# Strassen's seven products for the first of the gMLP's four down projections

## The chip, the cores and the metric

One program runs on one core of a Trainium2 chip. The metric is the device time of one execution in microseconds (us); a lower number is better. TensorE is called PE in the profile, VectorE DVE, ScalarE ACT, GpSimd POOL and the engine that issues most loads SP.

## What is computed

The reference is a trunk of two layers for 512 tokens of width 1024. Each layer is a feed-forward block (FFN), a mixer, a second FFN and a gated input embedding, with a layer norm after each. The mixer of the second layer is the gMLP, the only part that the change touches:

```python
def gmlp_mixer(x, w_in, b_in, vn_g, vn_b, ws, bs, w_out):
    u, v = jnp.split(jax.nn.gelu(x @ w_in + b_in, approximate=False), 2, axis=-1)
    v = layer_norm(v, vn_g, vn_b).reshape(B, NB, GM_BLOCK, GM_GROUPS, GM_GDIM)
    ...
    s = jnp.einsum('gts,bnsgc->bntgc', ws_m, v) + bs.T[:, :, None]
    return (u * s.reshape(B, S, GM_WIDTH)) @ w_out
```

`u` and `v` are 512 x 2048, `w_out` is 2048 x 1024, and all data is float32.

## The kernel before, in words

**Arithmetic.** A float32 product is made of three fp32r matmuls: each operand is split into a high part (an ACT copy, `whi`, `hh`, `fhi`) and a rest (a DVE subtraction, `wlo`, `hl`, `flo`), and `mm3` multiplies high by high, high by low and low by high. One matmul takes a 128 x 128 stationary tile and a 128 x 512 moving tile.

**The gMLP.** First `v` is computed for all tokens into the tile `gvf` (128 partitions x 4 token blocks x 2048 features), with its gelu and its norm. Then 16 blocks b of 128 features follow. For each of them PE does the spatial product (`spatial`, psum `sps`, 16 small matmuls) and the projection of u (`gate_u`, psum `gups`, 24 matmuls, one block ahead). DVE puts the spatial product's scale and bias together (`gadd`, then four instructions into `gs`), splits the next but one block of `gvf` (`gvl` or `gv`), multiplies `gs` by `guf`, the gelu of u, and ACT and DVE split the product into `hh` and `hl` (`gated`). After blocks 3, 7, 11 and 15 `down` multiplies the four blocks just made by four row tiles of `w_out`: for each of four token blocks two psum banks (`dps`), four features blocks and `mm3`, which are 4 x 2 x 4 x 3 = 96 matmuls. DVE adds the banks to the residual `xt` (eight instructions of 128 x 512).

**Weights.** The class `Weights` holds the order of the weight tiles (`W.order`, made by `gm_weights`). A tile is 128 x 1024: a projection tile u_b, or a row tile of `w_out`. Two of them come in one load of 1 MB on SP's queue (`load`, L162) into one of three raw buffers (`RAW_BUFS = 3`). `fill` splits the next tiles in order into slots, four of the kind "main" and two of the kind "extra"; `stage_kinds` gives every tile its kind, by its place in groups of six. A slot comes free when PE has used its tile (`release`), so a split is written five or six tiles ahead of its use, and the place of `release` in the code is the place of the split in the queues of ACT and DVE. A load is written right behind the split that used up a raw buffer. With `low="dma"` the low part is not made by DVE: ACT writes minus the high part (L196), and a DMA on POOL's queue adds the raw tile to it (L197).

ACT, DVE, POOL and SP each take their instructions in the order of the code, and an instruction that waits holds those behind it.

**Strassen's products elsewhere.** The FFN and the mLSTM mixer already do their down projections as seven products of half-size blocks (`Group`, `Weights.forms`). A weight form is a sum or difference of quarter blocks of two raw loads, made in place on DVE (`t2` and `t1`, two instructions of 128 x 1024 each), then split. A feature form is made in place in the feature tile and split into `fhi` and `flo`. A `Group` has `form`, which makes the next feature form, `product`, which multiplies one feature form by one weight form (2 x 2 x 3 = 12 matmuls into two banks `gps`), and `add`, which adds the two banks to `xt` (two DVE instructions). There are two pairs of banks, used in turn, and products 2, 4, 5 and 6 are accumulated into a pair that holds an earlier one, so the add of product r - 2 is done before product r.

Of the kernel before, what the change touches and what calls it, by code (L numbers as in the profile page):

```python
# [16 lines left out]
P = 128  # L17
# [220 lines left out]
def hybrid_trunk(ctx: ExitStack, tc, x, p, ln_g, ln_b, ffn1_wgu, ffn1_wd, ffn2_wgu, ffn2_wd,  # L238
# [130 lines left out]

    def stage_kinds(first):  # L370

        n = len(W.order) - first
        for i in range(n):
            extra = i % 6 >= 4 if i < n // 6 * 6 else i >= n - 2
            W.order[first + i] = ("extra" if extra else "main",) + W.order[first + i][1:]

    def ml_weights():
        win, wout = ml_w_in[0], ml_w_out[0]
        first = len(W.order)
        for h in range(HEADS):  # L380
# [7 lines left out]
            if h:  # L388
# [3 lines left out]
                j0, j1 = W.add_load(kp(wout)[:, k:k + 2, :], 3), W.add_load(kp(wout)[:, k + 2:k + 4, :], 3, "gb")  # L392
                left, right = ((slice(None), slice(None), slice(c, c + 512)) for c in (0, 512))
                down_w = W.forms("", (j0, left), (j0, right), (j1, right), (j1, left))
# [9 lines left out]
    def gm_weights():  # L404
        win, wout = gm_w_in[0], gm_w_out[0]
        first = len(W.order)
        for c in range(4):
            add_wide(win, GW + c * 512)
        for b in range(16):
            if b in (0, 15):  # L410
                W.add((kp(win)[:, :, b * P:(b + 1) * P], [slice(None)]))
            elif b % 2:
                W.add((w_cols(win, b * P), cols2))
            if b and b % 4 == 0:
                add_rows(wout, b - 4, 4)
# [314 lines left out]
    class Group:  # L730
# [5 lines left out]
        def __init__(self, h, pool, first=False):  # L736
            self.h, self.pool, self.half = h, pool, h.shape[1] // 2
# [5 lines left out]
        def form(self):  # L743

            def a(i, j):
                m = self.half
                return self.h[:, m * j - m:m * j, (i - 1) * 256:i * 256]
# [16 lines left out]
        def product(self):  # L764
# [5 lines left out]
            for e, ps in enumerate(self.banks[r % 2]):  # L770
                for k in range(self.half):
                    mm3(ps, [a[:, k, e * P:(e + 1) * P] for a in f], [a[:, k] for a in w],
# [429 lines left out]
    def gmlp():  # L1202
        with stage_pool("extra", EXTRA) as extra, stage_pool("gm_parts") as near, stage_pool("ghpool", 4) as hpool, \
                stage_pool("gm") as mp:
# [109 lines left out]
            def gated(s, uf):  # L1314
                vec.tensor_mul(s, s, uf)
                h = new_h(hpool)
                split(h[0], h[1], s)
                return h
# [5 lines left out]
            for b in range(16):  # L1324
                if b in (0, 14):
# [10 lines left out]
                hs.append(gated(ss.popleft(), us.popleft()))  # L1336
                if ahead and b < 14:
                    W.release(low="dma")
                elif b == 15:
                    W.release()  # L1340
                if b % 4 == 3:
                    down(hs, b == 3, Norm(1, 1) if b == 15 else None)
                    hs = []
# [150 lines left out]
```

## Time and profile before

| | us |
|---|---|
| median of three runs (2232.39 to 2232.61) | 2232.42 |
| the profiled execution's own time | 2232.51 |
| its span, from the first to the last instruction | 2230.8 |
| PE busy in the span | 2220.3 |
| DVE busy | 1526.0 |
| ACT busy | 913.9 |
| POOL busy | 101.8 |

PE begins the projection of u_0 at 1621.2 us of the span, and the last matmuls of u_15 start at 1788.6. The rows of a timeline give the start, the busy time, the engine, the line, out<-in and the count. A DVE or ACT instruction's busy time overlaps the next one's start by some 0.1 us, so in a full queue the distance of two starts is the cost of one. What stands in brackets is how long the engine had been idle and what it waited for.

### The profile page before, as it was taken

To read this page: it belongs to the slowest core of one execution; us is meant where nothing else is said; L and a number is where in the kernel's file an instruction comes from. 1 tells how busy PE (TensorE), PEld (TensorE's weight loads), DVE (VectorE), ACT (ScalarE), POOL (GpSimd) and SP (SyncE) were. 2 spreads that over 40 slices of the span, in tenths; PEclk is the share of its full clock that TensorE was granted. 3 is DMA by queue.
4 is the path that set the end of the run, shared out by engine and by line. 5 is a ranking of instruction groups with operands and counts; after the bars stand their busy time and mean duration, and the time that the engine had idled before them with its cause. 6 is when DMAs were issued, how large, how long until landed. Compare 5 with 4: busy or idle time off the path is not lost.

```text
span 2230.8 us, 26548 instructions
## 1 busy us (share of the span) xinstructions
PE 2220.3 (100%) x10589; PEld 1864.0 (84%) x10589; DVE 1526.0 (68%) x2240; ACT 913.9 (41%) x1298; POOL 101.8 (5%) x135
## 2 busy tenths in 40 slices
PE   9999999999999999999999999999999999999998
PEld 8888888888888888888889888888888888888887
DVE  5666667777776786666687666666666578666677
ACT  4333336454646533333255333334343453333332
POOL 1000000111101100000000000000010100000000
PEclk9999999999999999999999999999999999999999
DMA  7422323466847443332233422223355443332221
GB/s 231 130 93 88 95 85 100 100 149 135 166 107 161 123 139 126 95 104 67 95 123 122 133 86 87 93 87 109 106 142 142 104 151 123 122 113 85 85 85 57
DMA packets 202723, 253.56 MB, mean 114 GB/s; under 512 B 5812, under 2 KB 156468, under 8 KB 202600
## 3 DMA queue, kind: packets, MB, share of 16 engines
q1 hardware_dynamic: 168080, 211.83, 29.5%
q0 software_dynamic: 27904, 25.35, 7.9%
q10 hardware_dynamic: 6616, 14.69, 2.0%
q8 instruction: 83, 1.36, 0.2%
q14 instruction: 40, 0.33, 0.0%
HBM read 224.58 MB, written 2.11 MB: 102 GB/s over the span
## 4 chain that ended last, share of the span: by engine, by line
PE 99%; ACT 1%; DVE 0%; issue 0%; DVEq 0%; POOL 0%; POOLq 0%
PE fps L269 13%; PE fps L270 13%; PE fps L268 13%; PE gps L270 7%; PE gps L269 7%; PE gps L268 7%; PE dps L269 3%; PE dps L268 3%; PE dps L270 3%; PE gups L268 1%; PE vps L268 1%; PE zps L268 1%; PE zps L270 1%; PE vps L270 1%; PE gvps L268 1%; PE gups L269 1%
## 5 line engine op out<-in xcount | busy, mean ns | idle before, releaser
L268 PE MATMUL fps<-xh,whi 128*128 128x512 f32 x1312 | 510.7, 389 | 0.0
L269 PE MATMUL fps<-xl,whi 128*128 128x512 f32 x1312 | 510.5, 389 | 0.0
L270 PE MATMUL fps<-xh,wlo 128*128 128x512 f32 x1312 | 510.4, 389 | 0.0
L199 DVE TENSOR_TENSOR wlo<-wraw,whi 128x1024 fp32r<-128x1024 f32 (+1 forms) x286 | 345.4, 1218 | 149.5 <-ACT whi L193 147.8
L193 ACT ACTIVATE whi<-wraw 128x1024 fp32r<-128x1024 f32 (+1 forms) x334 | 346.5, 1048 | 185.8 <-PE fps L269 81.6
L199 DVE TENSOR_TENSOR wlo<-wquarter,whi 128x1024 fp32r<-128x1024 f32 (+1 forms) x140 | 156.5, 1118 | 218.2 <-ACT whi L193 218.2
L268 PEld LDWEIGHTS fps<-xh,whi 128*128 128x128 f32 x1312 | 246.3, 188 | 51.2
L269 PEld LDWEIGHTS fps<-xl,whi 128*128 128x128 f32 x1312 | 246.3, 188 | 51.1
L270 PEld LDWEIGHTS fps<-xh,wlo 128*128 128x128 f32 x1312 | 246.2, 188 | 51.0
L193 ACT ACTIVATE whi<-wquarter 128x1024 fp32r<-128x1024 f32 (+1 forms) x140 | 136.3, 974 | 279.8 <-PE gps L270 209.0
L270 PE MATMUL gps<-whi,flo 128*128 128x512 f32 x588 | 229.3, 390 | 0.0
L268 PE MATMUL gps<-whi,fhi 128*128 128x512 f32 x588 | 229.3, 390 | 0.0
L269 PE MATMUL gps<-wlo,fhi 128*128 128x512 f32 x588 | 229.2, 390 | 0.0
L593 DVE TENSOR_TENSOR xt<-xt,gps 128x512 f32<-128x512 f32 x282 | 180.3, 680 | 0.5 <-PE gps L270 0.5
L817 ACT ACTIVATE sg<-fps 128x512 f32<-128x512 f32 x80 | 47.9, 598 | 228.4 <-PE fps L270 228.4
L273 ACT ACTIVATE fhi<-h 128x512 fp32r<-128x512 f32 (+1 forms) x140 | 80.5, 581 | 142.9 <-DVE h L755 54.4
L269 PEld LDWEIGHTS gps<-wlo,fhi 128*128 128x128 f32 x588 | 110.4, 188 | 23.5
L268 PEld LDWEIGHTS gps<-whi,fhi 128*128 128x128 f32 x588 | 110.4, 188 | 23.3
L270 PEld LDWEIGHTS gps<-whi,flo 128*128 128x128 f32 x588 | 110.4, 188 | 23.3
L274 DVE TENSOR_TENSOR flo<-h,fhi 128x512 fp32r<-128x512 f32 (+1 forms) x140 | 87.2, 634 | 42.9 <-ACT fhi L273 42.9
L563 POOL TENSOR_TENSOR rs<-rs,eps_pow 128x1 f32<-128x1 f32 x32 | 20.6, 643 | 1556.4 <-DVE rs L562 1556.4
L466 ACT ACTIVATE xf<-xps,cols 128x128 f32<-128x128 f32 x160 | 59.8, 453 | 52.5 <-PE xps L461 52.5
(289 smaller groups left out, 3736.4 us busy)
## 6 DMA issues: line engine op xcount, KB each, us to landing
wraw<-in_ffn_wgu_dram SPq DMA_DIRECT2D x79, 1024.0 KB, 6.0
wquarter<-in_ffn_wd_dram SPq DMA_DIRECT2D x64, 512.0 KB, 3.7
wraw<-in_ml_w_in_dram SPq DMA_DIRECT2D x24, 1024.0 KB, 5.5
wlo<-wraw POOLq DMA_DIRECT2D x48, 512.0 KB, 6.5
wraw<-in_gm_w_in_dram SPq DMA_DIRECT2D x15, 1024.0 KB, 5.7
wraw<-in_ffn_wgu_dram SPq DMA_DIRECT2D x17, 512.0 KB, 4.0
wraw<-in_ffn_wd_dram SPq DMA_DIRECT2D x8, 1024.0 KB, 4.9
wraw<-in_ml_w_out_dram SPq DMA_DIRECT2D x8, 1024.0 KB, 4.9
```

Of the source, the lines that this page charges most:

```text
L193: self.nc.scalar.activation(hi[:, s], src[:, s], AF.Copy)
L199: self.nc.vector.tensor_sub(lo[:, s], src[:, s], hi[:, s].bitcast(F32))
L268: mm(ps, st[0], mv[0], start=start, stop=False, skip_group_check=more)
L269: mm(ps, st[0], mv[1], start=False, stop=False, skip_group_check=more)
L270: mm(ps, st[1], mv[0], start=False, stop=stop, skip_group_check=more)
L273: sca.activation(hi, src, AF.Copy)
L274: vec.tensor_sub(lo, src, hi.bitcast(F32))
L466: sca.activation(xf[:, k], ps[:, k], AF.Identity, scale=col("ln_g", norm.at + 4 * g + k), bias=col("ln_b", norm.at + 4 * g + k))
L563: pool.tensor_tensor(rs[:, 1:2], rs[:, 0:1], eps_pow, op=OP.pow)
L593: vec.tensor_add(dst, dst, ps)
L817: sca.activation(sg, ps, AF.Silu)
```

## The change

The first `down` of the gMLP, that of blocks 0 to 3, is replaced by a `Group` of seven products that are spread over blocks 4 to 7 (`GM_STEPS`: 2, 2, 2 and 1). The gated features of blocks 0 to 3 are written back to their place in `gvf` in float32 and not split there. The seven feature forms are made from `gvf`; since `gvf` has the tokens as rows and the features as columns, `Group` gets the flag `by_tokens`, which changes the indices alone. In `gm_weights` the four row tiles of the first group go out and seven weight forms of two loads of `w_out` come in, behind u_5 (two), u_6 (two), u_7 (two) and u_8 (one). They are called f0 to f6 here, their products p0 to p6, and the two loads j0 and j1. In blocks 6 and 7 `gated` comes after the products ("late"), and the features of every third and fourth block are split into the tiles of the forms' pool, which takes the place of half of the pool `ghpool`. The other three `down` stay. `stage_kinds` gives the last four tiles of the stage their kinds in another way.

```diff
     def stage_kinds(first):
         n = len(W.order) - first
         for i in range(n):
-            extra = i % 6 >= 4 if i < n // 6 * 6 else i >= n - 2
+            extra = i % 6 >= 4 if i < n - 4 else i >= n - 2
...
+    def two_row_forms(w, kind="raw"):
+        j0, j1 = W.add_load(w[:, :2], 3), W.add_load(w[:, 2:], 3, kind)
+        left, right = ((slice(None), slice(None), slice(c, c + 512)) for c in (0, 512))
+        return W.forms("", (j0, left), (j0, right), (j1, right), (j1, left))
...
-            if b and b % 4 == 0:
+        tiles = W.order[at:]
+        del W.order[at:]
+        for b, tile_b in enumerate(tiles):
+            W.order.append(tile_b)
+            k = (b - 1) // 4 - 1
+            if b > 4 and k < GM_GROUPS:
+                if b % 4 == 1:
+                    down_w = deque(two_row_forms(kp(wout)[:, 4 * k:4 * k + 4, :]))
+                for _ in range(GM_STEPS[(b - 1) % 4]):
+                    W.order.append(down_w.popleft())
+            if b % 4 == 0 and b > 4 * GM_GROUPS:
                 add_rows(wout, b - 4, 4)
...
-            def gated(s, uf):
+            def gated(b, s, uf):
+                if b < 4 * GM_GROUPS:
+                    dst = vf[:, :, b * P:(b + 1) * P]
+                    vec.tensor_mul(dst, s.rearrange("p (t c) -> p t c", t=TB), uf.rearrange("p (t c) -> p t c", t=TB))
+                    return
                 vec.tensor_mul(s, s, uf)
-                h = new_h(hpool)
+                if b % 4 < 2:
+                    h = new_h(hpool)
+                else:
+                    h = [fpool.tile([P, 2, 256], F32R, name=n, tag=n).rearrange("p t c -> p (t c)") for n in ("fhi", "flo")]
                 split(h[0], h[1], s)
...
+            def step():
+                group.add()
+                group.product()
+                W.release(low="dma")
+                group.form()
...
             for b in range(16):
+                if group is not None:
+                    group.add()
...
-                hs.append(gated(ss.popleft(), us.popleft()))
+                late = group is not None and b >= 4 * GM_GROUPS and b % 4 >= 2
+                if not late:
+                    gated(b, ss.popleft(), us.popleft())
...
+                if group is not None:
+                    for _ in range(GM_STEPS[b % 4]):
+                        step()
+                if late:
+                    gated(b, ss.popleft(), us.popleft())
                 if b % 4 == 3:
-                    down(hs, b == 3, Norm(1, 1) if b == 15 else None)
-                    hs = []
+                    if group is not None:
+                        group.add()
+                        group = None
+                    if b < 4 * GM_GROUPS:
+                        group = Group(vf[:, :, (b - 3) * P:(b + 1) * P], fpool, b == 3, True)
+                        group.form()
+                        group.form()
+                    else:
+                        down(hs, False, Norm(1, 1) if b == 15 else None)
+                        hs = []
```

On PE the change takes out the 96 matmuls `dps` behind u_4 and puts 84 matmuls `gps`, twelve for each product, behind u_5, u_6, u_7 and u_8. Three other queues change their order at the first blocks.

**SP, the loads of the gMLP's weights.** `gm_w_in` are projection tiles, `gm_w_out` the rows of the down projection. Before:

```order
L162 DMA wraw_12748<-in_gm_w_in_dram 128x8x256
L162 DMA wraw_12807<-in_gm_w_out_dram 128x2x1024
L162 DMA wraw_12898<-in_gm_w_out_dram 128x2x1024
L162 DMA wraw_13039<-in_gm_w_in_dram 128x8x256
L162 DMA wraw_13050<-in_gm_w_in_dram 128x8x256
```

Now:

```order
L162 DMA wraw_12751<-in_gm_w_in_dram 128x8x256
L162 DMA wraw_12810<-in_gm_w_in_dram 128x8x256
L162 DMA wraw_12901<-in_gm_w_out_dram 128x2x1024
L162 DMA wraw_13042<-in_gm_w_out_dram 128x2x1024
L162 DMA wraw_13090<-in_gm_w_in_dram 128x8x256
```

The load of u_5 and u_6 (`wraw_12810`) has come ahead of the two loads of `gm_w_out`. The second of these, j1 (`wraw_13042`), now stands where the load of u_5 and u_6 stood (`wraw_13039`): it goes into the buffer of u_3 and u_4 (`wraw_12751`), once u_4 is split.

**ACT, from the gelu of u_0 on.** `whi` is the high part of a weight tile, `guf` the gelu of u, `hh` the high part of a gated block. Before:

```order
L1280 ACTIVATE guf_12991<-gups_12966,cols_108 128x512
L273 ACTIVATE gvh_13010<-gvf_12282 128x512
L273 ACTIVATE gv_13031<-gvf_12282 128x512
L193 ACTIVATE whi_13035<-wraw_12748 128x1024
L193 ACTIVATE whi_13041<-wraw_12807 128x1024
L193 ACTIVATE whi_13045<-wraw_12807 128x1024
L196 ACTIVATE wlo_13046<-wraw_12807 128x1024
L193 ACTIVATE whi_13052<-wraw_12898 128x1024
L196 ACTIVATE wlo_13053<-wraw_12898 128x1024
L273 ACTIVATE hh_13058<-gs_13005 128x512
L1280 ACTIVATE guf_13087<-gups_13062,cols_108 128x512
```

Now:

```order
L1305 ACTIVATE guf_12994<-gups_12969,cols_108 128x512
L273 ACTIVATE gvh_13013<-gvf_12285 128x512
L273 ACTIVATE gv_13034<-gvf_12285 128x512
L193 ACTIVATE whi_13038<-wraw_12751 128x1024
L193 ACTIVATE whi_13044<-wraw_12810 128x1024
L193 ACTIVATE whi_13048<-wraw_12901 128x1024
L193 ACTIVATE whi_13052<-wraw_13042 128x1024
L1305 ACTIVATE guf_13082<-gups_13057,cols_108 128x512
L193 ACTIVATE whi_13085<-wraw_12810 128x1024
L196 ACTIVATE wlo_13086<-wraw_12810 128x1024
L273 ACTIVATE gvh_13109<-gvf_12285 128x512
L1305 ACTIVATE guf_13138<-gups_13113,cols_108 128x512
```

The four splits are now those of u_4, u_5, f0 and f1. f1 reads j1, `wraw_13042`, and behind it stands the gelu of u_2 (`guf_13082`).

**DVE, from the low part of u_4 on.** Before, up to the gated product of block 2:

```order
L199 TENSOR_TENSOR wlo<-wraw,whi 128x1024 x2
L1315 TENSOR_TENSOR gs<-gs,guf 128x512
L274 TENSOR_TENSOR hl<-gs,hh 128x512
L1315 TENSOR_TENSOR gs<-gs,guf 128x512
L274 TENSOR_TENSOR hl<-gs,hh 128x512
L1303 SCALAR_TENSOR_TENSOR gadd<-rsum,cols 128x128
L1307 SCALAR_TENSOR_TENSOR gs<-sps,cols,gadd 128x256
L1309 SCALAR_TENSOR_TENSOR gs<-sps,cols,gs 128x256
L1307 SCALAR_TENSOR_TENSOR gs<-sps,cols,gadd 128x256
L1309 SCALAR_TENSOR_TENSOR gs<-sps,cols,gs 128x256
L274 TENSOR_TENSOR gvl<-gvf,gvh 128x512
L1315 TENSOR_TENSOR gs<-gs,guf 128x512
```

Now, up to the weight form f2 (`t2` is L105 and L106):

```order
L199 TENSOR_TENSOR wlo<-wraw,whi 128x1024 x4
L1343 TENSOR_TENSOR gvf<-gs,guf 128x4x128 x2
L1328 SCALAR_TENSOR_TENSOR gadd<-rsum,cols 128x128
L1332 SCALAR_TENSOR_TENSOR gs<-sps,cols,gadd 128x256
L1334 SCALAR_TENSOR_TENSOR gs<-sps,cols,gs 128x256
L1332 SCALAR_TENSOR_TENSOR gs<-sps,cols,gadd 128x256
L1334 SCALAR_TENSOR_TENSOR gs<-sps,cols,gs 128x256
L274 TENSOR_TENSOR gvl<-gvf,gvh 128x512
L1343 TENSOR_TENSOR gvf<-gs,guf 128x4x128
L105 TENSOR_TENSOR wraw<-wraw 128x2x512
L106 TENSOR_TENSOR wraw<-wraw 128x2x512
L199 TENSOR_TENSOR wlo<-wraw,whi 128x1024
```

DVE makes four low parts in a row where it made two, and the forms f2 and, a block later, f3 (`t1`, L110 and L111) stand between the blocks' own work. The low parts of the first two feature forms come behind f3.

22 lines of the change are left out of this document (13 added, 9 removed).

## The prediction

> **What bounds the kernel now.** I read the page first (the engines' shares and the chain that ended last), then the busy time by stretches of the gMLP.
>
> ```profile
> PE 2220.3 (100%) x10589; PEld 1864.0 (84%) x10589; DVE 1526.0 (68%) x2240; ACT 913.9 (41%) x1298; POOL 101.8 (5%) x135
> PE 99%; ACT 1%; DVE 0%; issue 0%; DVEq 0%; POOL 0%; POOLq 0%
> 1632.00:1653.00 21.00, 21.00 (x110) 17.98 (x109) 17.86 (x34) 16.06 (x22) 4.15 (x4) 1.00 0.63 159
> 1652.40:1674.20 21.80, 21.80 (x98) 18.06 (x97) 7.84 (x11) 6.29 (x7) 1.60 (x2) 1.00 0.77 168
> 1674.20:1699.80 25.60, 25.60 (x130) 21.76 (x129) 18.87 (x35) 12.56 (x17) 3.28 (x3) 1.00 0.59 160
> ```
>
> PE bounds it: no gap, and the chain is 99% PE. The stretches are blocks 0 to 3, the `down` that goes, and blocks 4 to 7; their columns are length, busy PE, PEld, DVE, ACT and POOL, granted clock, DMA share, GB/s. PE is full in all three. DVE is busy 85% of the first (17.86 of 21.00) and 74% of the third, but 36% of the `down`: that stretch, in which DVE catches up, is what the change takes away. So I ask when DVE and ACT deliver what p0 to p6 need.
>
> **The matmuls saved.**
>
> ```profile
> 1652.14 0.39 PE L270 MATMUL gups<-xh,wlo 128*128 128x512 f32 x1
> 1674.13 0.28 PE L1300 MATMUL sps<-wsp,gvh 128*128 128x256 f32 x1
> 1675.00 0.45 PE L268 MATMUL gups<-xh,whi 128*128 128x512 f32 x1
> ```
>
> Between the last matmul of u_4 and the next spatial product lie 96 matmuls `dps`: 97 steps in 21.99 us, 0.227 each. 12 fewer give 12 x 0.227 = **-2.7 us**. A product is 2.7, a projection of 24 matmuls 5.4, a spatial product 0.9 (1675.00 - 1674.13). With nothing waiting, u_4 ends at 1652.4, the spatial product at 1653.3, u_5 at 1658.7, and there p0 could begin.
>
> **The load that ACT waits for.** The rows of SP, ACT and DVE around u_4's split, and landing times of 1 MB loads issued alone and beside one of POOL's adding DMAs:
>
> ```profile
> 1634.76 2.94 ACT L193 ACTIVATE whi<-wraw 128x1024 fp32r<-128x1024 f32 x3
> 1638.22 2.35 DVE L199 TENSOR_TENSOR wlo<-wraw,whi 128x1024 fp32r<-128x1024 f32 x2
> 1639.46 6.46 SPq L162 DMA_DIRECT2D wraw<-in_gm_w_in_dram  x2
> wraw<-in_gm_w_out_dram SPq DMA_DIRECT2D x1, 1024.0 KB, 4.9
> wraw<-in_gm_w_out_dram SPq DMA_DIRECT2D x1, 1024.0 KB, 7.9
> 1670.30 1.06 ACT L193 ACTIVATE whi<-wraw 128x1024 fp32r<-128x1024 f32 x1 [14.63 <-PE dps L270]
> 1646.85 0.45 PE L268 MATMUL gups<-xh,whi 128*128 128x512 f32 x1
> ```
>
> A split's high part is 2.94 / 3 = 0.98 on ACT in a row, 1.06 alone. Before, the load issued at 1639.46, behind u_4's low part, was that of u_5 and u_6 and nobody was in a hurry for it. Now j1 is issued there, and f1's split is the fourth in a row on ACT, which reaches it at 1637.7. With 4.9 (no DMA of POOL's is under way then) j1 lands at 1644.4 and f1's high part ends at 1645.4. Behind it on ACT stand the gelu of u_2 and the split of block 4's v; the gelu ends at about 1646.1, and u_4, which takes u_2's bank at 1646.85 (the last row), isn't held. On DVE f1's low part stands ahead of everything for blocks 0 to 3.
>
> **What DVE and ACT then do before p0.**
>
> ```profile
> 1640.49 0.68 DVE L1315 TENSOR_TENSOR gs<-gs,guf 128x512 f32<-128x512 f32 x1
> 1644.47 0.35 DVE L1303 SCALAR_TENSOR_TENSOR gadd<-rsum,cols 128x128 f32<-128x128 f32 x1
> 1646.75 0.68 DVE L274 TENSOR_TENSOR gvl<-gvf,gvh 128x512 fp32r<-128x512 f32 x1
> 1647.35 0.69 DVE L1315 TENSOR_TENSOR gs<-gs,guf 128x512 f32<-128x512 f32 x1
> 1648.73 0.69 DVE L274 TENSOR_TENSOR hl<-gs,hh 128x512 fp32r<-128x512 f32 x1 [0.70 <-ACT hh L273]
> 1648.61 1.05 ACT L193 ACTIVATE whi<-wraw 128x1024 fp32r<-128x1024 f32 x1
> 1649.56 1.04 ACT L196 ACTIVATE wlo<-wraw 128x1024 fp32r<-128x1024 f32 x1
> 1650.51 0.62 ACT L273 ACTIVATE gv<-gvf 128x512 fp32r<-128x512 f32 x1
> L105 DVE TENSOR_TENSOR wraw<-wraw x3: 1218/1219/1220, 464.9 to 660.5; 128x1024 f32<-128x1024 f32 x3
> L755 DVE TENSOR_TENSOR h<-h 128x512 f32<-128x512 f32 x12 | 8.3, 692 | 0.4
> ```
>
> From starts: a low part of a weight tile is (1640.49 - 1638.22) / 2 = 1.15; a block's scaling and bias (`gadd` and four) 1646.75 - 1644.47 = 2.28; a 128 x 512 instruction 0.6 in a queue, 0.69 alone. `t2` or `t1` is two of 1.2, the second behind the first, 2.4. The row of L105 is of the mLSTM's forms, of the same shape; the sums for feature forms (L755) are in place as here.
>
> DVE from 1645.45: f1's low part 1.15; blocks 0 and 1 gated 1.2; block 2's scaling, v split and gating 3.5; `t2` 2.4; f2's split, high part first (1.05 on ACT, DVE waiting), 2.2; block 3's scaling, v split and gating 3.5; `t1` 2.4; f3's split 2.2; the first feature form's low part 0.7. Sum 19.2, so it is there at 1664.6. p0's third matmul needs it, and would have run at 1659.2: PE waits **5.4**. Of that 3.8 is j1: without it f1's low part would follow the three others at 1641.6 (1638.2 + 3 x 1.15).
>
> **Products 1 to 5.** p0 and p1 end at 1669.6, the next spatial product and u_6 at 1676.0. DVE meanwhile: block 4's scaling and v, 2.9, to 1668.0; then its gating, at whose start ACT's line begins: `hh` 0.7 later, u_7's high and minus part, f4's high part, 4.2 in all by the rows above (1650.51 + 1.04 - 1647.35), to 1672.2. f4's low part 1.15; two sums for feature form 2, 1.3, its high part on ACT 0.65, its low part 0.6; then p0's add. p2 adds into p0's banks, so it waits for the first of the add's two instructions, which ends 0.7 later, at 1676.7: wait **0.7**, and p2 ends at 1679.4. DVE goes on with the second (0.6), f5's low part (1.15), form 3's (0.6) and the first of p1's add (0.7), to 1679.7: p3 waits **0.3** and ends at 1682.4; the next spatial product and u_7 take PE to 1688.7. DVE: the second of p1's add 0.6, block 5's scaling and v 2.9, to 1683.2; its gating up to f6's high part 4.2; f6's low part 1.15, one sum 0.7, form 4 1.25, the first of p2's add 0.7: 1691.2. p4 waits **2.5** and ends at 1693.9. Then 0.6, a sum 0.7, form 5 1.3 and the first of p3's add 0.7: 1694.5, p5 waits **0.6**. Together 9.5. These waits are one line of DVE and ACT that runs from 1645 to 1694 in which each piece waits for the one before; p5 starts where it ends.
>
> **p6 and the second `down`.**
>
> ```profile
> wlo<-wraw POOLq DMA_DIRECT2D x48, 512.0 KB, 6.5
> wraw<-in_gm_w_in_dram SPq DMA_DIRECT2D x1, 1024.0 KB, 9.9
> wlo<-wraw POOLq DMA_DIRECT2D x1, 512.0 KB, 10.2
> ```
>
> The load of the last two row tiles of group 2 needs the buffer of u_7 and u_8, free when POOL's DMA has made u_8's low part: minus part done 3.2 behind the start of block 5's gating (1650.51 - 1647.35), at 1686.4, plus 6.5, 1692.9. It lands after 4.9 to 9.9, and I take 7.9, since another adding DMA is under way: 1700.8. ACT holds form 6's high part behind these splits, and with 3.95 for high part, minus part, form and the first of p4's add, p6 can start at 1704.7; PE, with p5 to 1697.2, a spatial product and u_8, is there at 1703.6: **1.1** (0 to 3.1). The low part of the last row tile then comes by DMA at 1711.8 to 1715.5 (1705.3 plus 6.5 to 10.2), and the `down` asks for it at 1711.5: I take **1.0** (0 to 4), near the lower end, which most of those DMAs show.
>
> A page of the Trainium skill speaks against this term: "DMA: Bandwidth & Descriptors", section "Anatomy of one DMA — SWDGE (gpsimd) path", gives such a DMA 2.0 us plus its bytes over 436 GB/s, by which 512 KB would take 3.2 us. By the page's figure both terms of this part would be nothing and the sum 2.1 lower. The row, 48 such DMAs of this kernel, has twice the page's time, so the terms above go by the row.
>
> **The stage's end.** `stage_kinds` leaves the last row tile as "extra", and its slot comes free only with u_15, so its split now stands behind the gating of block 15, where before it was done three blocks ahead.
>
> ```profile
> 1789.02 0.69 ACT L1280 ACTIVATE guf<-gups,cols 128x512 f32<-128x512 f32 x1 [4.20 <-PE gups L270]
> 1792.12 1.04 ACT L193 ACTIVATE whi<-wraw 128x1024 fp32r<-128x1024 f32 x1
> 1793.19 1.23 DVE L199 TENSOR_TENSOR wlo<-wraw,whi 128x1024 fp32r<-128x1024 f32 x1 [0.26 <-ACT whi L193]
> ```
>
> In the place of this split (of a later tile) its low part would be done at 1794.4. u_15 ends at 1788.95, the `down` needs the tile 19 matmuls later, at 1793.25: **1.2** (0.5 to 1.5).
>
> **Sum.** -2.7 + 9.5 + 1.1 + 1.0 + 1.2 = +10.1 on the profiled execution's 2232.51, which is 0.09 over the median: **2242.5**. What else the change adds (six more adds, three more weight splits, four sums) lies in DVE's line already or in the `down` of groups 2 to 4, where DVE is two thirds idle.
>
> **Rivals.**
> - *All of it is hidden*, not slower: 2232.5 - 2.7 = 2229.8, within 0.2%, which is about what a measurement can tell from no change here. For it: the FFN does such products with PE full. Against it: there each product has a projection to itself, here two share one, in a stretch with DVE at 74 to 85%. It decides at p0: DVE's line would have to be 5.4 shorter there and 9.5 by p5. 0.11.
> - *j1 holds nobody* (it is there in time) and the rest stays: 3.8 less, 2238.7. Against it: the place of j1 behind u_4's split on SP. 0.10.
> - *PE slows after its wait.* No row before has PE idle that long, and the granted clock is 1.00 in every stretch. If p0 and p1 ran at half pace, 24 matmuls would cost 5.4 more; the waits at p2, p3 and p4 (3.5) would take most of that up, so +1.9 at most, 2244.4. "TensorE: Matmul & The Clock Gate", in "Part 1: The HAM clock gate" of the Trainium skill, says that an idle window of some 3.4 us halves PE's clock until a busy one has passed. 0.09.
> - The forecast itself: 0.70.
>
> Slower by over 0.2% (over 2236.9) are the forecast, the second rival and the third, 0.89, with 0.02 taken off for waits much shorter than I worked out: 0.87. Within 0.2% are the first and half of those: 0.12. The saving is 0.12%, so faster by over 0.2% needs a gain that no row shows: 0.01. The range takes the lower ends of the last three terms (2239.7 with 0, 0 and 0.5) and the second rival (2238.7, and 2235.9 with those ends too): 2236.5. Above, it takes p6 and the `down` at 3.1 and 3.0: 2246.5.
>
> **What would show it.** Right: PE idle 5 to 6 us ahead of the first `gps` of the gMLP, released by DVE `flo`; ACT idle about 6.7 us ahead of f1's `whi`, released by the DMA; an idle of 2 to 3 ahead of p4; about 1 at the fourth row tile of the last `down`. Wrong: PE without gaps there, f1's high part before 1642, or waits after p1 that sum to under 2.

## The result and the profile after

The changed kernel takes 2249.48 us, the median of four runs (2248.76 to 2250.74), against 2232.40 for four runs of before on the same chip: a ratio of 1.0077, 95% interval 1.006 to 1.0095. It is slower by 17.1 us. The forecast was slower by 10.1, and the range ended at 2246.5, so the direction was right and the size was not. The profiled execution took 2249.45, its span is 2247.7.

The page of the changed kernel, the engines' shares and the chain that ended last:

```profile
PE 2224.9 (99%) x10577; PEld 1864.9 (83%) x10577; DVE 1543.8 (69%) x2262; ACT 916.2 (41%) x1302; POOL 101.2 (5%) x133
PE 95%; DVE 1%; DMA 1%; ACT 1%; issue 1%; POOL 0%; DVEq 0%; ACTq 0%; POOLq 0%; SPq 0%
```

The busy time by stretches, with the columns of the prediction: blocks 0 to 3 with u_5, blocks 4 to 7 with the seven products, and the second `down`.

```profile
1632.00:1659.00 27.00, 27.00 (x140) 22.91 (x138) 20.89 (x35) 11.67 (x16) 1.61 (x1) 1.00 0.40 87
1659.00:1709.20 50.20, 42.20 (x181) 33.35 (x180) 33.55 (x54) 25.84 (x35) 6.55 (x6) 0.93 0.58 121
1709.20:1736.70 27.50, 24.07 (x98) 19.21 (x98) 12.61 (x21) 7.52 (x8) 3.15 (x2) 0.94 0.77 172
```

PE has gaps in the second and third stretch, 8.0 and 3.4 us, and in both its granted clock is below 1. The gaps are these, by the timeline of PE (the rows that have a wait in brackets); they are all that the timeline has from block 0 to the end of the gMLP:

```profile
1663.99 0.80 PE L268 MATMUL gps<-whi,fhi 128*128 128x512 f32 x1 [4.80 <-ACT fhi L273]
1692.09 0.47 PE L268 MATMUL gps<-whi,fhi 128*128 128x512 f32 x1 [1.29 <-DVE xt L612]
1695.34 0.47 PE L268 MATMUL gps<-whi,fhi 128*128 128x512 f32 x1 [0.28 <-DVE xt L612]
1706.24 0.47 PE L268 MATMUL gps<-whi,fhi 128*128 128x512 f32 x1 [1.51 <-DVE xt L614]
1709.39 0.50 PE L268 MATMUL dps<-whi,hh 128*128 128x512 f32 x1 [0.16 <-DVE xt L614]
1714.19 0.50 PE L268 MATMUL dps<-whi,fhi 128*128 128x512 f32 x1 [0.43 <-ACT fhi L273]
1717.54 0.79 PE L269 MATMUL dps<-wlo,fhi 128*128 128x512 f32 x1 [2.84 <-DMA wlo<-wraw]
1808.66 0.50 PE L268 MATMUL dps<-whi,fhi 128*128 128x512 f32 x1 [0.28 <-ACT whi L193]
1809.92 0.50 PE L269 MATMUL dps<-wlo,fhi 128*128 128x512 f32 x1 [0.76 <-DVE wlo L199]
```

The first four are p0, p4, p5 and p6, the next three the second `down`, the last two the last `down`. Behind the 4.80 and behind the 2.84 PE runs at half pace. By stretches of two us:

```profile
1666.00:1668.00 2.00, 2.00 (x6) 1.57 (x5) 1.82 (x5) 0.00 (x0) 0.00 (x0) 0.50 0.00 0
...
1670.00:1672.00 2.00, 2.00 (x11) 1.64 (x10) 0.69 (x1) 2.00 (x4) 0.00 (x0) 1.00 0.00 0
...
1716.00:1718.00 2.00, 0.46 (x1) 0.47 (x2) 0.06 (x1) 0.00 (x0) 0.00 (x0) 0.84 1.42 184
1718.00:1720.00 2.00, 2.00 (x6) 1.52 (x6) 0.69 (x1) 0.00 (x0) 0.00 (x0) 0.50 1.41 169
```

PE is full in 1666 to 1668 and in 1718 to 1720, both at a clock of 0.50, but only 6 matmuls overlap these 2 us, where 11 do in the row with 1.00. By their starts a matmul takes 0.43 us there and 0.23 elsewhere.

The account, from starts of PE against the starts that it would have without a wait:

| place | forecast | measured |
|---|---|---|
| 12 matmuls less | -2.7 | -2.7 (reckoned, not measured alone) |
| p0 to p5: delay at p5's start | 9.5 | 9.95 |
| p6 | 1.1 | 1.8 |
| second `down` | 1.0 | 5.9 |
| the stage's end | 1.2 | 1.5 |
| later start of the stage in this execution | 0 | 0.3 |
| sum | 10.1 | 16.75 |

The profiled executions differ by 2249.45 - 2232.51 = 16.94. The second `down` is read so: p6 starts at 1706.24 and the next spatial product at 1736.65, 30.4 later, where 12 matmuls and 96 in a row would take 24.5. By the brackets the waits are 0.16 + 0.43 + 2.84 = 3.4. By the distances of the starts, less the usual 0.23, the three cost 0.3, 0.6 and 3.1, together 4.0, since a matmul behind a wait is itself slower to start the next; the eight matmuls at half pace cost 1.6 more, and 0.3 is left. The end is read from the gelu of u_15: from its start (1804.40, and 1789.02 before) to the end of the span are 443.3 us, and 441.8 before.

### The profile page after: what moved, and what is told of

Same layout as the page of the kernel before. It is cut to its first block, busy times and chain, and to the rows that moved or that the text cites. A ratio compares the mean times of both kernels' runs of the same rounds, so it can differ in the third digit from the quotient of the medians.

```text
span 2247.7 us, 26554 instructions
## 1 busy us (share of the span) xinstructions
PE 2224.9 (99%) x10577; PEld 1864.9 (83%) x10577; DVE 1543.8 (69%) x2262; ACT 916.2 (41%) x1302; POOL 101.2 (5%) x133
## 4 chain that ended last, share of the span: by engine, by line
PE 95%; DVE 1%; DMA 1%; ACT 1%; issue 1%; POOL 0%; DVEq 0%; ACTq 0%; POOLq 0%; SPq 0%
PE fps L270 13%; PE fps L268 13%; PE fps L269 13%; PE gps L270 7%; PE gps L269 7%; PE gps L268 7%; PE dps L269 3%; PE dps L270 2%; PE dps L268 2%; PE vps L268 1%; PE zps L268 1%; PE zps L270 1%; PE vps L270 1%; PE gvps L270 1%; PE gvps L268 1%; PE zps L269 1%
## 5 line engine op out<-in xcount | busy, mean ns | idle before, releaser
L199 DVE TENSOR_TENSOR wlo<-wraw,whi 128x1024 fp32r<-128x1024 f32 (+1 forms) x291 | 351.1, 1218 | 158.7 <-ACT whi L193 157.8
L268 PE MATMUL gps<-whi,fhi 128*128 128x512 f32 x616 | 241.7, 392 | 7.9 <-ACT fhi L273 4.8
L270 PE MATMUL gps<-whi,flo 128*128 128x512 f32 x616 | 241.4, 392 | 0.1
L269 PE MATMUL gps<-wlo,fhi 128*128 128x512 f32 x616 | 241.2, 392 | 0.0
L268 PEld LDWEIGHTS gps<-whi,fhi 128*128 128x128 f32 x616 | 116.3, 189 | 33.8 <-ACT fhi L273 5.2
L270 PEld LDWEIGHTS gps<-whi,flo 128*128 128x128 f32 x616 | 116.2, 189 | 25.4 <-DVE flo L274 0.8
L269 PEld LDWEIGHTS gps<-wlo,fhi 128*128 128x128 f32 x616 | 116.2, 189 | 24.7
```

The costliest lines, as they stand in the source:

```text
L199: self.nc.vector.tensor_sub(lo[:, s], src[:, s], hi[:, s].bitcast(F32))
L268: mm(ps, st[0], mv[0], start=start, stop=False, skip_group_check=more)
L269: mm(ps, st[0], mv[1], start=False, stop=False, skip_group_check=more)
L270: mm(ps, st[1], mv[0], start=False, stop=stop, skip_group_check=more)
```

## The experiments

The theory: a line of DVE and ACT work that starts with the late load j1 holds p0 to p6; the second `down` waits for an adding DMA; the stage's end for the kind of a tile. The rivals are in the expectations. Each run is compared with runs of before on the same chip, whose medians lay between 2232.40 and 2232.52; ratios stand with their 95% intervals.

### The second form taken from the first load

```diff
-        return W.forms("", (j0, left), (j0, right), (j1, right), (j1, left))
+        made = W.forms("", (j0, left), (j0, right), (j1, right), (j1, left))
+        if f1_of_j0:
+            def first():
+                return W.raws[j0][left], (j1,)
+            W.in_place.add(first)
+            made[1] = made[1][:2] + (first,)
+        return made
```

> Form f1 is split from j0's left half where it should be j1's, so that its split doesn't wait for j1 (the second product then has a wrong weight form; nothing else is left out). My theory: j1's late landing is the head of the line of DVE and ACT, 3.8 us of it. f1's low part then follows the three others at about 1642, PE waits about 1.2 at p0 (and not 5), the clock isn't halved there, and all that follows on the line comes 3.8 earlier: 2249.5 - 3.8 = 2245.7 (2245 to 2246.5). The waits behind p5 stay as they are. Rival, the DVE work alone sets the line and PE would find the next late operand at once: less than 1 us gained.

Measured: 2245.46 us (2245.18 to 2245.68), 1.0058 [1.0043, 1.0073], 4.0 less than the changed kernel. PE at p0 and at the fourth row tile of the second `down`:

```profile
1660.12 0.50 PE L268 MATMUL gps<-whi,fhi 128*128 128x512 f32 x1 [0.96 <-ACT fhi L273]
1661.46 0.50 PE L270 MATMUL gps<-whi,flo 128*128 128x512 f32 x1 [0.61 <-DVE flo L274]
...
1713.11 0.50 PE L269 MATMUL dps<-wlo,fhi 128*128 128x512 f32 x1 [2.34 <-DMA wlo<-wraw]
```

p0 waits 1.57 in all where it waited 4.80 and a little more, and the gelu of u_15 comes 4.3 earlier (1800.09). The forecast had put 3.8 of p0's wait down to j1, and that holds for the line as a whole. At p0 itself some 5.7 are gone, the half pace with them, but p2 and p4 wait longer here (0.65 and 2.14, where p2 did not wait and p4 waited 1.29).

### The rows' low parts by DVE

```diff
                 group.product()
-                W.release(low="dma")
+                W.release()
```

> The tiles split in the seven steps (row tiles 0, 2 and 3 of the next down, and u_10) get their low part from DVE and not by POOL's adding DMA. My theory: the wait at the fourth row tile (2.8 us) and the half clock behind it (1.7) go, and the load of the last two row tiles lands earlier for the DMAs that are gone (about 1 us at p6); DVE gets three low parts of 1.15 in the line, of which one falls ahead of p5: 2249.5 - 4.5 - 1 + 1 = 2245 (2243.5 to 2246). Rival, DVE's line is the bound everywhere: each low part costs its 1.15, 2249 to 2252.

Measured: 2245.01 us (2244.47 to 2246.24), 1.0057 [1.0042, 1.0072], 4.5 less. PE from p4 to the second `down`:

```profile
1692.71 0.47 PE L268 MATMUL gps<-whi,fhi 128*128 128x512 f32 x1 [2.07 <-DVE xt L612]
1697.09 0.47 PE L268 MATMUL gps<-whi,fhi 128*128 128x512 f32 x1 [1.40 <-DVE xt L612]
1713.95 0.50 PE L268 MATMUL dps<-whi,fhi 128*128 128x512 f32 x1 [0.70 <-ACT fhi L273]
```

The wait for the DMA is gone, and so is the half pace behind it; p6 doesn't wait either. p4 and p5 wait 1.9 more, since DVE now has the low parts to do, and the `down` 0.3 more for a feature. By the rows the gain is 1.51 + 0.16 + 2.84 + 1.6 - 1.9 - 0.3 = 3.9, by the medians 4.5.

### Both at once

The two edits together.

> The changed kernel with both single edits at once: the second weight form taken from the first load's half (so the products are not the reference's) and the next down's low row parts by DVE instead of POOL's adding DMAs. Alone they gave 2245.5 (-4.0) and 2245.0 (-4.5). If the first product's wait and the row tiles' wait are two separate terms, they add: 2249.5 - 8.5 = 2241.0 (2240.3 to 2241.7). Rival: the stage between them is one line of DVE work, which takes back what the first product gains once DVE also carries four more low parts of 1.23 us: 2242.5 to 2243.5, with waits at the fifth and sixth product (2.1 and 1.4 us in the second run) longer than there.

Measured: 2240.31 us (2239.74 to 2241.02), 1.0036 [1.0023, 1.0049]. The two terms add (8.5 were expected, 9.2 came), and the rival, by which DVE takes one of them back, does not hold here: p4 and p5 wait 1.70 and 1.41, together no longer than 2.07 and 1.40. p0 waits 0.97 and 0.61 here, nearly as in the first run (0.96 and 0.61), but here the clock falls to 0.50 behind it, from 1661 to 1664.5, and there it did not.

### The kinds of the last tiles

```diff
-            extra = i % 6 >= 4 if i < n - 4 else i >= n - 2
+            extra = i % 6 >= 4
```

> The last four tiles of the gMLP's weights get their kinds by place in groups of six, like all others, so the last row tile is main and is split blocks ahead of its use. My theory: the 1.5 us that the last down loses at its fourth row tile go: 2248.0 (2247.7 to 2248.3). Rival, the tile's features (block 15's gating) are as late as its weights: under 0.4 gained.

Measured: 2250.8 us (2250.35 to 2253.34), 1.0084 [1.0069, 1.0099]. A miss. The waits at the last `down` are gone, but the next FFN begins with these (PE's timeline):

```profile
1830.40 0.39 PE L268 MATMUL sup<-xh,whi 128*128 128x256 f32 x1 [2.25 <-ACT whi L193]
1831.82 0.58 PE L270 MATMUL sup<-xh,wlo 128*128 128x256 f32 x1 [0.84 <-DVE wlo L199]
```

A row of SP's queue in that time:

```profile
1778.98 53.18 SPq L162 DMA_DIRECT2D wraw<-in_ffn_wgu_dram  x5
```

PE has a clock of 0.50 from 1831 to 1837, and five loads of the FFN are drawn out to 1832. From u_15's gelu to the end are 447.8 us, against 441.8 before: the end of this version costs 6.0. So the kinds of the stage's last tiles reach into the next stage. That the whole is only 1.3 longer than the changed kernel has another reason: from u_0 to u_15 this execution is 2.8 shorter, mainly since the second `down` waits only 1.91 for its DMA and no half pace follows. The edit touches no tile there, so that term differs from run to run, and why stays open. That this must be so for any other choice of kinds was the rival in the next run.

```diff
-            extra = i % 6 >= 4 if i < n - 4 else i >= n - 2
+            extra = i % 6 >= 4 if i < n - 5 else i >= n - 2
```

> The changed kernel with the kinds of the gMLP's last five weight tiles set as before the change (only the last two of 51 are extra, i % 6 >= 4 now holds for i < n - 5; nothing is left out). My theory of the end: the 0.28 + 0.76 + what follows them, 1.5 us in all, come from the last projection tile being extra, which holds the buffer that a row tile of the last down needs. So the two waits at the last down go, the FFN's first tiles do not come late, and the time is 2249.5 - 1.5 = 2248.0 (2247.4 to 2248.6). Rival, from the run with extra by i % 6 alone: the wait moves to the FFN's first weight tiles whatever is done to the kinds, and the time stays at 2249.5 or above.

Measured: 2248.33 us (2246.86 to 2249.52), 1.0071 [1.0057, 1.0085], 1.15 less than the changed kernel; the four runs spread over 2.7 us, more than the gain, so the trace tells more than the median. PE near u_15 has only these two waits, and none in the last `down` or at the FFN's start:

```profile
1797.60 0.38 PE L1325 MATMUL sps<-wsp,gv 128*128 128x256 f32 x1 [0.37 <-ACT gv L273]
1798.32 0.33 PE L1326 MATMUL sps<-wsp,gv 128*128 128x128 f32 x1 [0.34 <-DVE gv L274]
```

From u_15's gelu to the end are 441.8 us again, so the whole 1.5 of the end is the kind of u_15's tile. 0.7 of it comes back as these two waits.

### The first step with one product

```diff
-    GM_GROUPS, GM_STEPS = 1, (2, 2, 2, 1)
+    GM_GROUPS, GM_STEPS = 1, (1, 2, 2, 2)
```

> The seven products stand 1, 2, 2, 2 over blocks 4 to 7 and not 2, 2, 2, 1; the weight tiles' order moves with them, so the fourth early split is u_6 and f1 comes a block later. My theory: neither j1 nor the form f3 stands ahead of p0 now, so p0 doesn't wait and the line up to p5 is at least 3.8 shorter; the wait at the second down's row tiles stays or grows, since p6 stands right ahead of it: 2243 (2239 to 2246). Rival, the sum of DVE's work in blocks 4 to 7 is the bound wherever the products stand: 2248 to 2251.

Measured: 2241.52 us (2241.20 to 2242.84), 1.0042 [1.0026, 1.0059]. p0 doesn't wait at all, though ACT still stands 4.13 us for j1: f1 and f3 are no longer ahead of p0. Up to the second `down` PE's waits are now at p2, at p4, at p6 and at that `down`, and the low part's DMA is in time:

```profile
1674.05 0.47 PE L268 MATMUL gps<-whi,fhi 128*128 128x512 f32 x1 [3.28 <-DVE xt L612]
1688.49 0.47 PE L268 MATMUL gps<-whi,fhi 128*128 128x512 f32 x1 [0.77 <-DVE xt L612]
1702.56 0.47 PE L268 MATMUL gps<-whi,fhi 128*128 128x512 f32 x1 [1.96 <-DVE xt L614]
1706.47 0.50 PE L268 MATMUL dps<-whi,hh 128*128 128x512 f32 x1 [0.93 <-DVE xt L614]
```

All four are released by DVE's adding to `xt`. This is the largest gain that one line gave (8.0), and it leaves a question: do the products wait for the order of DVE's work, or for its sum?

### DVE's order or its sum

The next kernel has one product in the first step, the kinds with `n - 5`, and one add placed before the late gating:

```diff
                 if late:
+                    group.add()
                     gated(b, ss.popleft(), us.popleft())
```

> The whole computation, in another order: one product in the first step instead of the last (1, 2, 2, 2), the kinds of the last tiles as before the change, and in the third block the adding of the product's bank placed ahead of the gating of the next feature block (add first, then gate). From the run with 1, 2, 2, 2 alone (2241.5): the end gives back 1.5; the wait of 1.96 on the bank's adding, which stood on DVE behind the low part of the gated features, loses the 0.69 and the ACT part ahead of it, 1.3, and the 0.93 at the down loses about as much as it has: 2241.5 - 1.5 - 1.3 - 0.7 = 2238.0 (2236.8 to 2239.5). Rival: these waits are for PE's own product to end, not for DVE's order, and only the end is given back: 2240.0.

Measured: 2241.14 us (2239.53 to 2241.65), 1.0037 [1.0025, 1.005]. A miss. p6 no longer waits, but the `down` behind it does, and the busy time by stretches shows the clock there:

```profile
1705.37 0.50 PE L268 MATMUL dps<-whi,hh 128*128 128x512 f32 x1 [1.97 <-DVE xt L614]
```

```profile
1706.00:1708.00 2.00, 2.00 (x7) 1.55 (x6) 1.71 (x3) 2.00 (x4) 1.59 (x1) 0.53 1.16 271
```

The two waits of 1.96 and 0.93 have become one of 1.97 a little later, and behind this one PE runs at half pace, which costs what the order and the end had gained.

The next run takes work off DVE in this reordered kernel: the four weight sums go to POOL, which is nearly idle.

```diff
-        vec = self.nc.vector
+        vec = sums or self.nc.vector
...
-                    down_w = deque(two_row_forms(kp(wout)[:, 4 * k:4 * k + 4, :]))
+                    down_w = deque(two_row_forms(kp(wout)[:, 4 * k:4 * k + 4, :], sums=pool))
```

> As the reordered kernel, with the four weight sums of the gMLP's group (two for the third form, two for the fourth, 1.22 us each on DVE) issued on POOL. If DVE's line of work is what the products wait for, the wait of 3.28 at the third product and the half pace behind it (about 2 us) go, up to 4.9 of sums leaves the line, and the time is 2238.0 - 4.3 = 2233.7 (2232.5 to 2236). If DVE is not the bound there, but the landing of the second load or ACT behind the sums, it stays within 0.7 of the reordered kernel; if POOL takes over three times DVE's 1.22 us a sum, ACT's high part waits for POOL in DVE's place and the time is the same or up to 3 longer.

Measured: 2241.50 us (2241.06 to 2243.36), 1.0042 [1.003, 1.0055]. A miss. The time is that of the expectation's last case, but POOL's sums take 2 to 2.7 times DVE's and not over three, and the reason is another. The rows of POOL and of DVE beside each other:

```profile
1657.65 3.03 POOL L110 TENSOR_TENSOR wraw<-wraw 128x1024 f32<-128x1024 f32 x1
1660.76 2.68 POOL L111 TENSOR_TENSOR wraw<-wraw 128x1024 f32<-128x1024 f32 x1
```

```profile
1657.91 0.48 DVE L1334 SCALAR_TENSOR_TENSOR gs<-sps,cols,gs 128x256 f32<-128x256 f32 x1
1658.31 2.92 DVE L274 TENSOR_TENSOR gv<-gvf,gv 128x512 fp32r<-128x512 f32 x1
1661.16 2.83 DVE L1343 TENSOR_TENSOR gvf<-gs,guf 128x512 f32<-128x512 f32 x1
```

POOL takes 2.4 to 3.3 us for a sum that takes DVE 1.22. In that time DVE's `gv` and `gvf` instructions, 0.68 elsewhere, take 2.92 and 2.83: each ends some 0.55 us after POOL's sum beside it, about its own length. The instruction that reads a PSUM bank keeps its 0.48 beside POOL's sum. So the sums still lie on DVE's line, with more than twice their length, and p0, which did not wait before, waits 3.22 for the low part of its features. The Trainium skill says so in "SBUF — State Buffer", section "SBUF: two separate sides": GpSimd and a VectorE instruction with two inputs in SBUF take turns at one port pair, held for a whole instruction. This trace agrees: 2.92 and 2.83 for the two that have both inputs in SBUF, 0.48 for the one that reads PSUM.

Then the order, in earnest: features and adds first, weight tiles last, block 6 gated beside block 7. The release that stood behind the gating of a block moves, in blocks 4 to 7, behind the products.

```diff
             def step():
-                group.add()
                 group.product()
-                W.release(low="dma")
                 group.form()
+                if group.next_product < 7:
+                    group.add()
...
                 if group is not None:
+                    if b % 4 == 3:
+                        W.release()
                     for _ in range(GM_STEPS[b % 4]):
                         step()
-                if late:
-                    gated(b, ss.popleft(), us.popleft())
+                    if not late:
+                        W.release(1 + GM_STEPS[b % 4], low="dma")
...
+                if late and b % 4 == 3:
+                    for i in (b - 1, b):
+                        gated(i, ss.popleft(), us.popleft())
+                if late:
+                    W.release(GM_STEPS[b % 4] + (b % 4 == 2), low="dma")
```

> The whole computation, with one product in the first step, the kinds as before, and DVE's line put in the order of need: after each product first the next feature form, then the adding of the product, and the filling of weight tiles only at the block's end; block 6 is gated beside block 7. At stake in the reordered kernel (2241.1) are 3.3 us of wait and 2.0 of half pace at the third product, 0.7 at the fifth, 2.0 and 1.7 at the down: 9.7. If these came from the order, the waits left are some 1.6 at the fourth product, 0.5 at the sixth and 1.1 at the down: 2241.1 - 9.7 + 3.2 = 2234.6 (2233 to 2237). Rival: DVE's work in sum is the bound between the first product and the down (42 of 52 us busy, with 7 us of its idle time spent waiting for ACT in its own chains), so a wait taken from one product comes back at the next: 2239 to 2241.

Measured: 2239.37 us (2238.49 to 2241.04), 1.0032 [1.0021, 1.0044]. The rival's number. No product waits any more, but block 6's spatial product does, for a bank that DVE has not read, a projection waits 0.52 for its low part, and the `down` waits in four pieces of 0.2 to 0.9:

```profile
1677.38 0.36 PE L1325 MATMUL sps<-wsp,gvh 128*128 128x256 f32 x1 [2.15 <-DVE gs L1334]
1704.06 0.47 PE L268 MATMUL dps<-whi,hh 128*128 128x512 f32 x1 [0.84 <-DVE xt L614]
```

The busy time by stretches, from block 4's gating to the `down`:

```profile
1663.30:1703.20 39.90, 37.23 (x166) 30.24 (x164) 31.41 (x50) 20.04 (x26) 4.10 (x4) 0.96 0.46 112
```

DVE is busy 31.4 of these 39.9 us. Up to 1698 its idle times are all of this kind, 0.7 to 1.1 in a split in which it waits for ACT's high part:

```profile
1673.49 2.36 DVE L199 TENSOR_TENSOR wlo<-wraw,whi 128x1024 fp32r<-128x1024 f32 x2 [1.13 <-ACT whi L193]
```

So DVE and the short hand-overs to ACT in its own chains fill the time; reordered, the wait comes out at another place. The line still begins with the late load: ACT stands 4.09 us for j1, and DVE 2.76 for the high part behind it, ahead of this stretch:

```profile
1645.68 1.06 ACT L193 ACTIVATE whi<-wraw 128x1024 fp32r<-128x1024 f32 x1 [4.09 <-DMA wraw<-in_gm_w_out_dram]
```

No run takes that load out of this order, so what it costs here stays open.

Another way to take work off DVE is to give three of the weight forms' low parts to ACT and an adding DMA:

```diff
-        for _, make in made:
+        for _, make in made[:last]:
             self.in_place.add(make)
...
-                    down_w = deque(two_row_forms(kp(wout)[:, 4 * k:4 * k + 4, :]))
+                    down_w = deque(two_row_forms(kp(wout)[:, 4 * k:4 * k + 4, :], last=4))
```

> As the kernel with the forms first, with the low parts of the fifth, sixth and seventh weight forms made by ACT's negated copy and POOL's adding DMA instead of DVE: 3 x 1.23 = 3.7 us off DVE, 3 x 1.04 on ACT, three more adding DMAs. If DVE's work is still what the products wait for, 1 to 2.5 us shorter than with the forms first (2233 if that is 2234.6). Rival, by what the changed kernel's second down showed (10.5 us from issue to landing with loads under way): a form's low part lands after its product is due, with a wait of 2 to 4 us and half pace behind it, 2 to 5 us longer than with the forms first.

Measured: 2243.93 us (2243.72 to 2245.32), 1.0054 [1.004, 1.0068], 4.6 longer than without. It is the rival's size, though not at the products. PE's large waits, and an ACT row:

```profile
1690.34 0.50 PE L270 MATMUL gups<-xh,wlo 128*128 128x512 f32 x1 [2.52 <-DMA wlo<-wraw]
1706.77 0.76 PE L268 MATMUL dps<-whi,hh 128*128 128x512 f32 x1 [5.69 <-DVE xt L614]
```

```profile
1700.73 1.06 ACT L193 ACTIVATE whi<-wraw 128x1024 fp32r<-128x1024 f32 x1 [6.82 <-DMA wraw<-in_gm_w_out_dram]
```

The projection waits 2.52 where it waited 0.52, with two of the forms' DMAs issued behind its own, and ACT stands 6.82 us at the split of the last row tiles, whose load came late; behind it on ACT waits the `gv` that DVE needs, and DVE's adding stands behind that.

The last run leaves DVE's sums out of the kernel with the forms first, and changes nothing else:

```diff
         def t2():
-            vec.tensor_sub(raw(b12), raw(b22), raw(b12))
-            vec.tensor_add(raw(b11), raw(b12), raw(b11))
+            if sums:
+                vec.tensor_sub(raw(b12), raw(b22), raw(b12))
+                vec.tensor_add(raw(b11), raw(b12), raw(b11))
             return raw(b11), ()
```

and the same in `t1`, with `sums=False` for the gMLP's group.

> The kernel with the forms first (2239.4), with the four weight sums of the gMLP's group left out (the third and fourth forms are then made from plain blocks of w_out, so the products are not the reference's; their splits, loads and products all stay). It takes 4 x 1.22 = 4.9 us off DVE and nothing off any other engine. If DVE's work in sum is what the products wait for, the second pair (2.45, with the 1.13 that DVE waits for ACT behind it partly hidden) goes from the line between the first and the fourth product: the wait of 2.15 at block 6's spatial product and the half pace behind it (about 1.3) go and the wait of 0.84 at the down shrinks, so 2239.4 - 3.5 to 4.3 = 2235.5 (2234.8 to 2236.3). If the loads, the adding DMAs or ACT's chains set the waits, it stays within 1 of 2239.4.

Measured: 2232.54 us (2232.27 to 2233.53), 1.0001 [0.9992, 1.001]: 6.8 less than the kernel with the forms first, more than expected. PE's waits in the gMLP are these, and the clock is 1.00 in every stretch:

```profile
1698.72 0.50 PE L271 MATMUL dps<-wlo,hh 128*128 128x512 f32 x1 [0.36 <-DMA wlo<-wraw]
1701.22 0.51 PE L271 MATMUL dps<-wlo,fhi 128*128 128x512 f32 x1 [0.85 <-DMA wlo<-wraw]
1781.65 0.38 PE L1327 MATMUL sps<-wsp,gv 128*128 128x256 f32 x1 [0.36 <-ACT gv L275]
1782.37 0.33 PE L1328 MATMUL sps<-wsp,gv 128*128 128x128 f32 x1 [0.34 <-DVE gv L276]
```

4.9 us of DVE's work are worth 6.8 of the kernel's time. So DVE's line is the bound in blocks 4 to 7, in this order of the code: nothing was taken off any other engine. (ACT's high parts of two forms wait for these sums and start earlier without them, and the next load of `gm_w_out` goes out some 6 us earlier in the stage; the run doesn't tell these effects apart, all are of the sums.) ACT still stands 4.12 us for j1 here and DVE 2.80, so with the sums gone the late load alone holds no product. What is left of the waits, 1.9 by the brackets and 2.6 by the distances of the starts, takes back the 2.7 of the matmuls.

### What the group itself does not cost

```diff
-    GM_GROUPS, GM_STEPS = 1, (2, 2, 2, 1)
+    GM_GROUPS, GM_STEPS = 0, (2, 2, 2, 1)
```

All four `down` are plain here; the first of them adds to x without the factor ALPHA, in as many instructions.

> The changed kernel with no block group by the seven products (GM_GROUPS = 0): all four downs are plain, and what is left of the change is the split of the pool of gated features into two pools of two and the new rule for the kinds, which gives the same kinds as before when there is no group. My theory: nothing but the group's own waits and DMAs cost the 17.1 us, so 2232.5 (2232.0 to 2233.0). Rival: the two smaller pools make the gated features wait for a buffer, 0.5 to 2 us in the four downs, 2233.0 to 2240.

Measured: 2232.53 us (2232.26 to 2233.80), 1.0 [0.9991, 1.0009], and PE has no wait in the gMLP. The two smaller pools cost nothing; all 17 us belong to the group and to what its tiles shift.

No version beat the kernel before: the best that computes the reference is the one with the forms first, 7 us slower than before.

## Why the prediction was right in its direction and wrong in its size

**The mechanism at p0 to p5 held.** ACT reached f1's split early and stood 6.65 us for the load; the split began at 1644.64, where 1644.4 was forecast. p0's third matmul came at 1665.33 (forecast 1664.65), p4 at 1692.09 (1691.2), p5 at 1695.34 (1694.5). j1's part of it was measured at 4.0 against 3.8. Of the signs that it named, ACT's wait and the wait at the last `down` (0.28 + 0.76) came as forecast. p0 waited 4.80 and not 5 to 6, and what ended this wait was the high part of the feature form on ACT, which stands there behind f3's high part; the low part on DVE came only afterwards. At p4 it was 1.29 and not 2 to 3.

```profile
1644.64 1.06 ACT L193 ACTIVATE whi<-wraw 128x1024 fp32r<-128x1024 f32 x1 [6.65 <-DMA wraw<-in_gm_w_out_dram]
```

**The half pace.** The third rival's half pace came, but not its cost. Its working had 24 matmuls at half pace, 5.4 us, less 3.5 of later waits: +1.9 at most. Only part of p0 and p1 ran with 0.43 us a matmul where 0.23 is usual, some 2.4 us more in all, and the waits of 0.7, 0.3 and part of 2.5 that were forecast at p2, p3 and p4 were gone or shorter by as much, since DVE's line set the time anyway. It had been given 0.09, and its working asked only what p0's wait would do.

**The step that failed is "p6 and the second `down`".** It gave 1.1 and 1.0, and 1.8 and 5.9 were measured: the 1.8 lies within its bounds, so what failed is the term of the second `down`, 4.9 of the 7.0 us that the forecast was short. For the low part of the last row tile it took a wait of 1.0, "near the lower end, which most of those DMAs show", that is a DMA of 7.2 us; 6.5 would give 0.3 and 10.2 the 4.0. The 6.5 is the median over 48 DMAs of the whole kernel. This one was issued on POOL at 1706.96 and landed at about 1717.5, when PE's wait ended: 10.5 later. A load of the next projections, issued at 1706.5 and 11.7 us long, and two more adding DMAs were under way in that time, and the DMA share was 1.42 and 1.41 in the stretches from 1716 to 1720 (above). That these drew it out is likely and not shown: no run takes them away and leaves this DMA. The rows of SP's and of POOL's queue:

```profile
1694.38 12.47 SPq L162 DMA_DIRECT2D wraw<-in_gm_w_in_dram  x2
```

```profile
1706.96 0.86 POOL L197 DMA_DIRECT2D wlo<-wraw  x1 [1.56 <-ACT wlo L196]
1711.30 1.59 POOL L197 DMA_DIRECT2D wlo<-wraw  x1 [3.48 <-DVE gs L1334]
```

The prediction had the 10.2 row in hand, and its own bound of 4; it took the wrong end. With 10.2 from the start that it gave (1705.3) the wait would have come out at 4.0, near the 3.4 that the waits sum to. The second part of the failure is the half pace behind this wait, 1.6 us: no later wait is there to take it up, and no working had been done for it. The run with the low parts by DVE has both gone, and is 4.5 shorter.

**The stage's end** was 1.5 and not 1.2, within its bounds.

**The range** was too narrow above because it put only 3.0 of its bound of 4 at the `down` into the upper end and none of the half pace; with both it would have ended at 2249.1, and 2249.48 was measured.

**What the prediction did not ask**: whether DVE, at 85% in blocks 0 to 3 and 74% in blocks 4 to 7, could carry the group in any order. It names these shares against its first rival, and its line was worked out step by step and came out right, but as a chain started by a late load. With one product in the first step, so that the load no longer held p0, 6.9 us of waits were left up to the second `down`, of 11.3 before; the order alone moved them, and with 4.9 us of sums gone most of them went, although the load was as late as before.

Of the 6.8 that the sums were worth, most is wait: from the start of u_0 to the last matmul of the gMLP the two traces differ by 7.05, of which by the distances of the starts 4.9 are waits and some 1.9 half pace. What stays open is how much the late load costs in the kernel with the forms first, and why the adding DMA took 10.5.

## What to carry to other kernels

A step that trades PE's matmuls for sums and splits on the vector engine gains only where that engine has room in the same stretch: here 2.7 us of PE stood against four sums, three more weight splits and six adds, in blocks that had 15 to 26% of DVE free. Time a DMA by the row of a like one that ran beside the same traffic, not by the median of all. And price a wait on the bounding engine twice, once for its length and once for the clock behind it; the second price falls due only where no later wait takes it up.

## What the runs showed of the hardware

- **PE's clock can fall after a short wait.** Half pace followed all nine waits of 2.84 us and more that the traces have in the gMLP (up to 5.69), and also those of 2.67 and 2.34 (each with one of 0.4 shortly ahead), 2.25, 2.15 and 1.97, and once 0.97 and 0.61 with two matmuls between them. None followed a wait of 2.52, those of 1.96, 2.07, 2.12 and 2.14 at other places, or 0.96 and 0.61 at the same place in another run. It lasted some 3 to 7 us, at 0.43 us a matmul for 0.23. So between 1.6 and 2.5 us it hangs on something that these traces don't show. "TensorE: Matmul & The Clock Gate" in the Trainium skill ("Part 1: The HAM clock gate") gives an idle window of some 3.4 us, free-running; waits of about 2 that were enough are shorter than that.
- **POOL's sums of two tiles stretch DVE's instructions with two SBUF inputs**: 0.68 became 2.92 and 2.83, while POOL's own sums took 2.39 to 3.26.
- **An adding DMA of 512 KB** took 5.4 to 12.7 us between 1692 and 1726 of the changed kernel, with loads of 1 MB under way that took 11.7 and 13.2 us each.
